# Joined state and V products in a chunked recurrence, a later rotation, three more held-back units and a norm's sum on TensorE

## The chip, the core and the metric

The kernel runs on one core of one Trainium2 chip, in one launch. The metric is the device time of that core in microseconds (us), as the median of several runs. Five engines work beside each other, each in its own order: TensorE (PE, its weight loads PEld), VectorE (DVE), ScalarE (ACT), GpSimd (POOL) and SyncE (SP), whose queue issues the DMAs.

## The reference

Two layers, each a feed-forward block, a mixer of three kinds of heads, and a second feed-forward block, each followed by a layer norm. 16 learned tokens lead 512 input tokens, so 528 positions are computed. Cut to what the change touches:

```python
for l in range(2):
    h = layer_norm(alpha * h + 0.5 * swiglu(h, w_ff1_in, w_ff1_out))
    h = layer_norm(alpha * h + mixer(h))      # gated DeltaNet | RWKV-7 | retention
    h = layer_norm(alpha * h + 0.5 * swiglu(h, w_ff2_in, w_ff2_out))

def rwkv7_step(S, r, w, k, v, a, b):          # one token, 4 heads of 64 x 64
    S = S * w + outer(S @ a, b) + outer(v, k)
    return S, S @ r
y = head_group_norm(y) + (sum(r * k * r_k) * v)   # the bonus, then times a gate

q, k = rotary(q), rotary(k)                   # retention: x1*cos - x2*sin, x1*sin + x2*cos
```

## The kernel before

The 528 positions are cut into half 0 (272) and half 1 (256). Activations stand as 8 blocks of 128 channels by positions. A dense product is a *unit*: one weight tile of 1024 x 128 is loaded (`load_w`, L150: a DMA into `raw`, then ScalarE copies the high part and VectorE subtracts it from the raw value, giving `whl`), and `mm3` (L160) runs 24 passes, high x high, high x low and low x high for each of 8 blocks. A unit of half 1 has 256 columns, of half 0 272. A float32 product that isn't split this way shows as two passes in the trace. Feed-forward units are `gate`, `up` and `ffo`; input units of the mixer `rt`, `ba`, `qkv`, `rw`, `z`; output units `out`.

The mixer works on "supers" of two chunks of 64 positions (the first of a layer is one chunk of 16). `rwkv_pre` prepares operands, `inverse_base` and `inverse_levels` invert a triangular matrix, `rwkv_chain` (L911) is the serial part, and `rwkv_post` normalises. In a step of the chain for a chunk, `pR` takes the product of the state with kappa (`kr[..., 0]`) and, accumulated, of V with the upper part of `Am` (`pR<-UV,Am`); `R` is its copy; `pu` multiplies by the inverse; `pSr` updates the state; `pyr` takes the state with r (`kr[..., 1]`) and then U and V together with the other half of `Am`. ScalarE copies `pyr` into `yv`. The layer's first chunk has no state yet.

`rt` units 0 and 1 are retention's q and k: the product goes into a bank of psA, ScalarE copies it to `rq`, a matmul with a fixed matrix makes the rotated copy `rot` in psA's other bank, and VectorE and GpSimd combine both with the two tables `tab`, which a DMA brings after the product.

`layer_norm` (L189): GpSimd sums the 8 blocks into `acc`; `pmean` is a matmul with ones; VectorE subtracts the mean from four pairs of blocks; ScalarE squares them; VectorE and GpSimd add the squares into one block; `pvar` sums over channels; a short chain of VectorE steps makes the inverse root, and `prs` spreads it.

What sets the order: the program is written down half by half, and a scheduler puts each engine's instructions into one fixed order from priorities and durations of its own model; tiles of a pool (psA, psB: 2 banks, psC: 3, and rings of named buffers in `RINGS`, L78) hold a new user back until the last one has ended. An engine then runs its list in order. In layer 0 the first feed-forward of half 1 is split: `u[:h]` (L1196, h = 13) runs before the mixer's input units of half 0, the rest beside the half-0 mixer, which fills TensorE while the chain waits.

Of the kernel before, what the change touches and what calls it, by code (L numbers as in the profile page):

```python
# [12 lines left out]
AF = mybir.ActivationFunctionType  # L13
# [22 lines left out]

_C = {}
_n = 0
for _name, _w in (("id", 128), ("u2", 128), ("mneg", 128), ("lvl", 2 * 64), ("rm", 128), ("rm0", 32),
                  ("u", 128), ("rot", 128), ("b2", 128), ("hm", 4), ("bm", 2), ("g128", 4), ("g16", 4)):  # L40
    _C[_name] = (_n, _n + _w)
    _n += _w
# [17 lines left out]
def body(ctx, tc, xT, w1i, w1o, w2i, w2o, win, wba, wout, par, wsm, wupx, cst, tab, out):  # L60
# [15 lines left out]


    RINGS = {  # L78
        "ws": (276, 5), "acc": (NMAX, 2), "dg": (NMAX, 2),
        "p2": (2 * NMAX, 15), "p1": (264, 8), "i2": (512, 5), "xr": (256, 2), "i1": (256, 2), "c2": (512, 2), "c1": (256, 2),  # L80
        "ti": (4, 16), "tp": (4, 18), "s6": (24, 2), "tf": (24, 10),
    }

# [15 lines left out]
    def bank(pool, name="ps"):  # L99
        return pool.tile([128, 512], F32, tag="bank", name=name)  # L100
# [13 lines left out]
    def tt(e, o, a, b, op):  # L114
        e.tensor_tensor(out=o, in0=a, in1=b, op=op)  # L115
# [13 lines left out]
    def mm(o, l, r, start=True, stop=True):  # L129
        PE.matmul(o, lhsT=l, rhs=r, start=start, stop=stop)  # L130
# [36 lines left out]

    S = {}

    nh, off = list(NH), [0, 0]  # L170

    def hv_(hf):
# [16 lines left out]
    def layer_norm(hf, l, j, last=False):  # L189
# [14 lines left out]
        for k in range(0, 8, 2):  # L204
            stt(hv[:, k: k + 2], bc(pm[:, :n], 1, (128, 2, n)), -1.0 / 1024, hv[:, k: k + 2], ALU.mult, ALU.add)
            sq = ring("p2", 2, n, name="sq")
            act(sq, hv[:, k: k + 2], AF.Square)
            sqs.append(sq)
            if k == 2:
                tt(V if end else G, sqs[0], sqs[0], sq, ALU.add)  # L210
# [4 lines left out]
        tt(V, sq[:, 0], sq[:, 0], sq[:, 1], ALU.add)  # L215
        for i in range(4):
# [153 lines left out]
    def in_units(l):  # L370
# [81 lines left out]
        def rt(i):  # L452
            def run(hf, w):
                n = nh[hf]
                ps = bank(psA, "rt")[:, :n]
                mm3(ps, w, S["hl", hf], 8)
                d = keep(hf, "rt")[:, i, :n]
                if i < 2:
                    q = ring("ws", n, name="rq")
                    act(q, ps, AF.Copy)  # L460
                    pr = bank(psA, "rot")[:, :n]
                    mm(pr, cs["rot"], q)
                    tb = [ring("ws", n, name="tab") for _ in range(2)]
                    for j in range(2):
                        nc.sync.dma_start(out=tb[j], in_=tab[hf, :, 2 * i + j, :n])
                    tt(V, d, pr, tb[1], ALU.mult)
                    tt(G, q, q, tb[0], ALU.mult)
                    tt(G, d, d, q, ALU.add)
                elif i < 4:
                    act(d, ps, AF.Copy)  # L470
                else:
                    silu2(d, ps, n)
            return (win[l, 19 + i], 8, run)

        def zz(i):
# [15 lines left out]
    def inverse_base(dg, dw, nch, Cn):  # L491
# [9 lines left out]

        def M(c, h):
            r = slice(64 * c, 64 * c + Cn)
            return Mg[r, h, 64 * c: 64 * c + Cn] if h < 4 else Am[h % 2][r, 2 * c + (h - 4) // 2, :Cn]

        def at(t, off, ap):
            return bass.AP(tensor=t.tensor, offset=t.offset + off, ap=ap)
# [5 lines left out]
        for c in range(nch):  # L513
            r = slice(64 * c, 64 * c + Cn)
            o = c * 8 * HS
            nc.sync.dma_start(out=at(md, o, [[Cn, Cn], [HS, 4], [1, Cn]]), in_=Mg[r, :, 64 * c: 64 * c + Cn])
            for e in range(2):
                nc.sync.dma_start(out=at(md, o + (4 + e) * HS, [[Cn, Cn], [2 * HS, 2], [1, Cn]]),
                                  in_=Am[e][r, 2 * c: 2 * c + 2, :Cn])
# [271 lines left out]
    def rwkv_pre(hf, si, d, pool):  # L791
# [7 lines left out]
        def pc(ap):  # L799
            return ap.rearrange("p j (c t) -> p j c t", c=nch)  # L800
# [42 lines left out]
        bb = ta  # L843
        stt(bb, ta, 1.0, kap, ALU.add, ALU.mult)
        tt(V, bb, bb, rec, ALU.mult)
        yield

        bk = ring("p2", 2, 2 * nch, w, name="bk")
# [14 lines left out]
        rkp = kap  # L863
        tt(G, rkp, r_, kp, ALU.mult)
        pb = bank(pool, "pb")[:, : 2 * n].rearrange("p (j t) -> p j t", j=2)
        for j in range(2):
            mm(pb[:, j], S["rk2"][:, j], rkp[:, j])
        bv = two("bv")
        for c in range(nch):
            cc, cv = slice(c * Cn, c * Cn + Cn), slice((nch - 1 - c) * Cn, (nch - c) * Cn)  # L870
            tt(V, bv[:, :, cc], pb[:, :, cc], v_[:, :, cv], ALU.mult)
        yield

        Am = []
        w2 = 2 * w
        rmask = cs["rm"] if nch == 2 else cs["rm0"]
        bkc = bk.rearrange("p j (c b) t -> p j c (b t)", c=nch)

        pA = [bank(pool, "pAr")[:w2, : nch * 4 * Cn].rearrange("p (q i) -> p q i", q=2 * nch) for _ in range(2)]
# [31 lines left out]
    def rwkv_chain(hf, si, d):  # L911
        s, n, nch, Cn, w = SUPERS[hf][si]
        w2 = 2 * w
        Am, UV, kr, bkt = d["Am"], d["UV"], d["kr"], d["bkt"]
        yv = ring("c1", 4, 64, name="yv")
        d["yv"] = yv
        for c in range(nch):
            r = slice(64 * c, 64 * c + Cn)
            vr = slice(w, w + Cn) if c == 0 else slice(0, Cn)
            Sb, first = S["Sr"], not (hf or si)  # L920
            pR = bank(psC, "pR")[:, :256]
# [8 lines left out]
            act(R[r], pR[r], AF.Copy)  # L930
            yield
# [3 lines left out]
            py = bank(psC, "pyr")[:, :256].rearrange("p (h d) -> p h d", h=4)  # L935
            if not first:
                for j in range(2):
                    mm(py[r, 2 * j: 2 * j + 2].rearrange("p h d -> p (h d)"), kr[:, j, c, 1], Sb[:, j], j == 0, False)
# [5 lines left out]
            for j in range(2):  # L944
                for e in range(2):
                    h = 2 * j + e
                    mm(py[r, h], Am[e][:w2, 2 * c + j, Cn: 2 * Cn], UV[:w2, c, 64 * h: 64 * h + 64],
                       first, first or h == 3)
            pc4 = bc(d["pcm"][:, c].rearrange("p j e -> p (j e)"), 2, (128, 4, 64))
            S24 = Sb.rearrange("p j (e d) -> p (j e) d", e=2)  # L950
            if not first:
                tt(V, Sb, Sb, pS, ALU.add)
                tt(V, S24, S24, pc4, ALU.mult)
            else:
                tt(V, S24, pS.rearrange("p j (e d) -> p (j e) d", e=2), pc4, ALU.mult)
            act(yv[r], py[r], AF.Copy)
            yield

    def rwkv_post(hf, si, d):
# [21 lines left out]
        tt(V, S["rt", hf][:, 4:6, sl], y, pg, ALU.mult)  # L981
        yield


# [191 lines left out]
    for l in range(L):  # L1176
# [67 lines left out]
def _consts():  # L1244
# [17 lines left out]
    put("rm", np.concatenate([j64[:, None] < k[None, :], j64[:, None] <= k[None, :]], 1))  # L1262
# [107 lines left out]
```

## Time and profile before

| | |
|---|---|
| median of 3 runs | 2441.68 us (2435.64 to 2444.03) |
| the profiled execution | 2435.65 us, span 2433.9 us |
| mean granted TensorE clock | 0.987 |
| busy: PE, DVE, ACT, POOL | 97%, 74%, 51%, 12% of the span |
| matmul passes in the trace | 19834 |

The profile is of one execution. Busy time of an engine is the time in which at least one of its instructions runs; matmuls are pipelined, so a pass shown as 0.28 us can follow the last one after 0.12 us, and the distance between two starts is what a pass costs. A row of a timeline merges equal instructions that follow each other. A number in square brackets at the end of a row is the engine's idle time ahead of it, with the instruction that ended the wait. Some per cent of matmul records can be missing. The granted clock of TensorE has two levels, 1.00 (2.4 GHz) and 0.50 (1.2 GHz).

### The profile page before, as it was taken

How to read it: one execution, taken by the hardware profiler on the slowest of the kernel's cores; microseconds unless marked ns; L12 is line 12 of the kernel's file. 1: busy time of each engine (PE TensorE's matmuls, PEld its weight loads, DVE VectorE, ACT ScalarE, POOL GpSimd, SP SyncE). 2: the span in 40 equal slices, each digit the busy share in tenths (PEclk: the TensorE clock that was granted, in tenths of full speed). 3: DMA queues.
4: the chain of work that ended last, by engine and by line, in shares of the span. 5: the costliest groups of instructions: out<-in, count | busy, mean ns of one | idle time of the engine just before them, and what ended most of it. 6: DMA issues, size and time to landing. Idle time of an engine off the chain costs nothing. (4 is left out here: it accounts for less than half of the span.)

```text
span 2433.9 us, 51363 instructions
## 1 busy us (share of the span) xinstructions
PE 2360.8 (97%) x19834; PEld 2270.8 (93%) x19834; DVE 1812.2 (74%) x4315; ACT 1229.7 (51%) x2821; POOL 297.0 (12%) x484
## 2 busy tenths in 40 slices
PE   9999999997999999999999999999998999999997
PEld 9999999996999999999999999899998999999997
DVE  6668687867788756976657779976688886677667
ACT  5445555534566335554444555544556653445444
POOL 1001112101223000300000003220022220010002
PEclk9999999998999999999999999999999999999998
DMA  6655544433454625555555554344455445355554
GB/s 233 209 171 166 187 163 135 147 113 110 147 171 150 174 88 168 166 173 182 180 177 181 193 163 142 119 138 124 153 170 191 157 148 155 122 164 174 191 169 134
DMA packets 169819, 389.24 MB, mean 160 GB/s; under 512 B 63750, under 2 KB 79720, under 8 KB 168936
## 3 DMA queue, kind: packets, MB, share of 16 engines
q1 hardware_dynamic: 169576, 385.97, 49.3%
q8 instruction: 156, 2.56, 0.4%
q14 instruction: 87, 0.71, 0.1%
HBM read 372.04 MB, written 13.88 MB: 159 GB/s over the span
## 5 line engine op out<-in xcount | busy, mean ns | idle before, releaser
L127 ACT ACTIVATE whl<-raw 128x512 fp32r<-128x512 f32 x1384 | 780.2, 614 | 627.5 <-PE ffo L165 198.3
L115 DVE TENSOR_TENSOR whl<-raw,whl 128x512 fp32r<-128x512 f32 x1384 | 949.4, 717 | 105.0 <-ACT whl L127 92.1
L165 PE MATMUL gate<-hi,whl 128*128 128x256 f32 (+1 forms) x2816 | 552.7, 287 | 6.3 <-DVE m L118 4.7
L165 PE MATMUL up<-hi,whl 128*128 128x256 f32 (+1 forms) x2816 | 552.6, 287 | 2.0 <-ACT whl L127 1.0
L165 PE MATMUL ffo<-ghi,whl 128*128 128x256 f32 (+1 forms) x2816 | 532.2, 286 | 3.4 <-DVE h L118 3.3
L165 PEld LDWEIGHTS gate<-hi,whl 128*128 128x128 f32 x2816 | 449.5, 189 | 12.1 <-DVE m L118 5.5
L165 PEld LDWEIGHTS up<-hi,whl 128*128 128x128 f32 x2816 | 450.2, 189 | 6.4 <-ACT whl L127 1.1
L165 PEld LDWEIGHTS ffo<-ghi,whl 128*128 128x128 f32 x2816 | 441.0, 188 | 9.8 <-DVE h L118 4.5
L165 PE MATMUL gate<-lo,whl 128*128 128x256 f32 (+1 forms) x1408 | 402.6, 286 | 0.6 <-DVE lo L115 0.6
L165 PE MATMUL up<-lo,whl 128*128 128x256 f32 (+1 forms) x1408 | 402.8, 286 | 0.0
L165 PE MATMUL ffo<-glo,whl 128*128 128x256 f32 (+1 forms) x1408 | 399.1, 284 | 0.0
L165 PEld LDWEIGHTS up<-lo,whl 128*128 128x128 f32 x1408 | 265.8, 189 | 2.2 <-issue 0.5
L165 PEld LDWEIGHTS gate<-lo,whl 128*128 128x128 f32 x1408 | 265.6, 189 | 2.2 <-DVE lo L115 1.1
L165 PEld LDWEIGHTS ffo<-glo,whl 128*128 128x128 f32 x1408 | 264.9, 188 | 1.0 <-issue 0.4
L127 ACT ACTIVATE tanh<-gate 128x256 f32<-128x256 f32 (+1 forms) x176 | 68.2, 388 | 219.3 <-PE gate L165 218.9
L118 DVE SCALAR_TENSOR_TENSOR h<-ffo,h 128x256 f32<-128x256 f32 (+1 forms) x192 | 81.2, 427 | 109.7 <-PE ffo L165 108.8
L118 DVE SCALAR_TENSOR_TENSOR m<-tanh,gate 128x256 f32<-128x256 f32 (+1 forms) x176 | 74.5, 423 | 116.0 <-ACT tanh L127 115.1
L165 PE MATMUL qkv<-hi,whl 128*128 128x272 f32 (+1 forms) x768 | 152.5, 290 | 1.9 <-ACT rk L127 1.9
L115 DVE TENSOR_TENSOR m<-m,up 128x256 f32<-128x256 f32 (+1 forms) x176 | 74.6, 424 | 96.9 <-PE up L165 96.4
L165 PEld LDWEIGHTS qkv<-hi,whl 128*128 128x128 f32 x768 | 122.5, 188 | 5.3 <-ACT rk L127 2.7
L165 PE MATMUL qkv<-lo,whl 128*128 128x272 f32 (+1 forms) x384 | 109.4, 285 | 0.0
L165 PE MATMUL out<-yhi,whl 128*128 128x256 f32 (+1 forms) x512 | 98.6, 291 | 7.4 <-DVE h L118 3.1
(326 smaller groups left out, 3221.4 us busy)
## 6 DMA issues: line engine op xcount, KB each, us to landing
raw<-w1i SPq DMA_DIRECT2D x176, 512.0 KB, 3.5
raw<-w2i SPq DMA_DIRECT2D x176, 512.0 KB, 3.4
raw<-win SPq DMA_DIRECT2D x116, 512.0 KB, 3.3
raw<-w1o SPq DMA_DIRECT2D x64, 512.0 KB, 3.3
raw<-w2o SPq DMA_DIRECT2D x64, 512.0 KB, 3.3
raw<-wout SPq DMA_DIRECT2D x32, 512.0 KB, 3.3
raw<-w1o SPq DMA_DIRECT2D x32, 384.0 KB, 3.1
raw<-w2o SPq DMA_DIRECT2D x32, 384.0 KB, 3.1
```

Of the source, the lines that this page charges most:

```text
L115: e.tensor_tensor(out=o, in0=a, in1=b, op=op)
L118: V.scalar_tensor_tensor(out=o, in0=a, scalar=s, in1=b, op0=op0, op1=op1)
L127: A.activation(out=o, in_=a, func=f, **kw)
L165: PE.matmul(ps, lhsT=w[:, a, k, :m], rhs=x[b][:, k, :n], start=(i == 0), stop=(i == 3 * nk - 1))
```

## The change

- **Recurrence.** `kr` holds kappa and r side by side, in the order (kappa, r) for chunk 0 and (r, kappa) for chunk 1, so that one product with the state gives 128 rows: 64 for `R` and 64 for y. The V product uses both halves of `Am` at once and accumulates into the same bank. ScalarE copies both parts out; `pyr` keeps only U's product, which VectorE adds to y. y and the bonus `bv` of the two chunks now stand in reversed order, which `rwkv_post` undoes in its last product. `Am` is masked chunk by chunk with shifted windows of a wider mask.
- **`rkp`**, the factor of the bonus, is made one step earlier.
- **Rotation.** The tables come in one DMA ahead of the unit's passes; the rotated product is written after the next unit's passes (`later`, `flush`) into a bank of psB.
- **Held-back units.** h = 10 for 13.
- **Last norm.** TensorE sums all eight blocks of squares for the last half of the last layer.
- **Rings.** `dg` one buffer for two, `c1` three for two, `rm` 64 columns wider.

```diff
-        "ws": (276, 5), "acc": (NMAX, 2), "dg": (NMAX, 2),
+        "ws": (276, 5), "acc": (NMAX, 2), "dg": (NMAX, 1),
...
+    def later(fn):
+        S.setdefault("later", []).append(fn)
+    def flush():
+        for fn in S.pop("later", ()):
+            fn()
...
+            if end:
+                for kk in range(2):
+                    for i in range(4):
+                        mm(pv[:w, i: i + 1], sq[:, kk, i * w: i * w + w], ones[:, 0:1], k + kk + i == 0, k + kk == 7 and i == 3)
+                continue
...
                 if i < 2:
                     q = ring("ws", n, name="rq")
                     act(q, ps, AF.Copy)
-                    pr = bank(psA, "rot")[:, :n]
-                    mm(pr, cs["rot"], q)
-                    tb = [ring("ws", n, name="tab") for _ in range(2)]
-                    for j in range(2):
-                        nc.sync.dma_start(out=tb[j], in_=tab[hf, :, 2 * i + j, :n])
-                    tt(V, d, pr, tb[1], ALU.mult)
-                    tt(G, q, q, tb[0], ALU.mult)
-                    tt(G, d, d, q, ALU.add)
+                    flush()
+                    def rotate():
+                        pr = bank(psB, "rot")[:, :n]
+                        mm(pr, cs["rot"], q)
+                        tt(V, d, pr, tb[:, 1], ALU.mult)
+                        tt(G, q, q, tb[:, 0], ALU.mult)
+                        tt(G, d, d, q, ALU.add)
+                    later(rotate)
...
-        tt(G, kr[:, :, :, 0], pc(kap), Pt[:, :, :, 0:Cn], ALU.mult)
-        tt(G, kr[:, :, :, 1], pc(r_), Pt[:, :, :, 1:], ALU.mult)
+        for c in range(nch):
+            tt(G, kr[:, :, c, c], pc(kap)[:, :, c], Pt[:, :, c, 0:Cn], ALU.mult)
+            tt(G, kr[:, :, c, 1 - c], pc(r_)[:, :, c], Pt[:, :, c, 1:], ALU.mult)
...
-            tt(V, a[:w2], pA[e], bc(rmask[:w2, : 2 * Cn], 1, (w2, 2 * nch, 2 * Cn)), ALU.mult)
+            for c in range(nch):
+                q2 = slice(2 * c, 2 * c + 2)
+                tt(V, a[:w2, q2], pA[e][:, q2], bc(rm[c][:w2, : 2 * Cn], 1, (w2, 2, 2 * Cn)), ALU.mult)
...
-            for j in range(2):
-                if not first:
-                    mm(pR[r, 128 * j: 128 * j + 128], kr[:, j, c, 0], Sb[:, j], True, False)
-                for e in range(2):
-                    h = 2 * j + e
-                    mm(pR[r, 64 * h: 64 * h + 64], Am[e][vr, 2 * c + j, :Cn], UV[vr, c, 64 * h: 64 * h + 64],
-                       first, first or e == 1)
+            if not first:
+                for j in range(2):
+                    mm(pR[:, 128 * j: 128 * j + 128], kr[:, j, c].rearrange("p a t -> p (a t)"), Sb[:, j], j == 0, False)
+            o, ka = (r, slice(0, Cn)) if first else (slice(0, 128), slice(0, 2 * Cn))
+            for h in range(4):
+                mm(pR[o, 64 * h: 64 * h + 64], Am[h % 2][vr, 2 * c + h // 2, ka], UV[vr, c, 64 * h: 64 * h + 64], first, first or h == 3)
             act(R[r], pR[r], AF.Copy)
+            if not first:
+                act(y, pR[ry], AF.Copy)
...
+            py = bank(psC, "pyr")[:, :256]
+            for h in range(4):
+                mm(py[ry, 64 * h: 64 * h + 64], Am[h % 2][ur, 2 * c + h // 2, ra], UV[ur, c, 64 * h: 64 * h + 64])
...
-            act(yv[r], py[r], AF.Copy)
+            if first:
+                act(y, py[ry], AF.Copy)
+            else:
+                tt(V, y, y, py[ry], ALU.add)
...
-            h = 13
+            h = 10
```

The order on TensorE at the end of the first feed-forward of half 1 in layer 0, before (`pot`, `pyt` and `pgate` are the mixer's tail, `pmean`, `pvar` and `prs` the norm of half 1, `out` the output units of half 0):

```order
L130 MATMUL pSr<-UV,rk 128x128 x2
L130 MATMUL pyr<-UV,Am 64x64 x4
L765 MATMUL pot<-cst,on 128x128 x4
L130 MATMUL pmean<-acc,ones 128x256
L130 MATMUL pvar<-ones,sq 64x1 x4
L973 MATMUL pyt<-cst,yn 128x128 x2
L130 MATMUL pgate<-sg,wsm 128x128 x2
L130 MATMUL prs<-diag,ones 128x256
L165 MATMUL out<-yhi,whl 128x272 x2
```

And now, from the last `ffo` pass on (between `pot` and this row stand 108 `ffo` passes):

```order
L165 MATMUL ffo<-ghi,whl 128x256
L130 MATMUL pmean<-acc,ones 128x256
L1003 MATMUL pyt<-cst,yn 128x128 x2
L130 MATMUL pgate<-sg,wsm 128x128 x2
L130 MATMUL pvar<-ones,sq 64x1 x4
L165 MATMUL out<-yhi,whl 128x272 x2
L165 MATMUL out<-ylo,whl 128x272
```

The mixer's tail now comes before `pvar`, and `prs` follows 27 `out` passes later. The same tail in layer 1 had 111 `ffo` passes between `pot` and `pyt` and none between `pgate` and `out`; now 7 `up` and 117 `ffo` passes stand there, and 27 `ffo` passes behind `pgate`.

A step of the recurrence on TensorE, in the half-0 mixer of layer 0, before (`pR` holds what the products leave, `Sr` the state, `UV` the u and v rows; `up` is the feed-forward of the other half):

```order
L130 MATMUL pR<-Sr,kr 64x128
L130 MATMUL pR<-UV,Am 64x64 x2
L130 MATMUL pR<-Sr,kr 64x128
L130 MATMUL pR<-UV,Am 64x64 x2
L165 MATMUL up<-hi,whl 128x256
```

And now, with the same neighbours on either side:

```order
L165 MATMUL up<-hi,whl 128x256 x2
L130 MATMUL pR<-Sr,kr 128x128 x2
L130 MATMUL pR<-UV,Am 128x64 x4
L165 MATMUL up<-lo,whl 128x256
L165 MATMUL up<-hi,whl 128x256 x2
```

The two blocks' state passes now stand together and ahead of all four UV passes, each twice as wide in its output. The row `pyr<-Sr,kr 64x128 x2`, which followed each later `pu` before, is gone. At the last norm the row `pvar<-ones,sq 64x1 x4` became `pvar<-ones,sq 64x1 x32`.

## Rows read from the trace of the kernel before

**Rows 1.** The page, busy time of each engine, share of the span, instructions

```profile
PE 2360.8 (97%) x19834; PEld 2270.8 (93%) x19834; DVE 1812.2 (74%) x4315; ACT 1229.7 (51%) x2821; POOL 297.0 (12%) x484
```

**Rows 2.** Windows: length, busy us (count) by engine, granted clock, DMA share, GB/s

```profile
550.00:600.00 50.00, 39.42 (x359) 36.21 (x358) 38.48 (x103) 21.75 (x53) 8.75 (x13) 0.93 0.38 126
...
1100.00:1150.00 50.00, 50.00 (x411) 50.00 (x410) 31.36 (x58) 22.86 (x45) 0.00 (x0) 1.00 0.55 179
```

**Rows 3.** Timeline of TensorE: start, length, line, out<-in, count, [idle before]

```profile
584.79 0.65 PE L130 MATMUL pyr<-Sr,kr 128*64 128x128 f32 x4
...
586.18 0.60 PE L130 MATMUL pSr<-UV,rk 128*128 128x128 f32 x4
586.72 0.68 PE L130 MATMUL pyr<-UV,Am 128*64 128x64 f32 x8
587.33 0.66 PE L765 MATMUL pot<-cst,on 128*128 128x128 f32 x4
587.82 0.62 PE L130 MATMUL pmean<-acc,ones 128*128 128x256 f32 x2
...
607.14 0.59 PE L165 MATMUL out<-ylo,whl 128*128 128x272 f32 x1 [2.35 <-DVE ylo L115]
```

**Rows 4.** The same for VectorE, same stretch

```profile
590.87 2.47 DVE L118 SCALAR_TENSOR_TENSOR h<-pmean,h 128x512 f32<-128x512 f32 x4
```

**Rows 5.** Timeline of TensorE in the rotation units of half 1, both layers

```profile
639.98 0.70 PE L130 MATMUL rot<-rq,cst 128*128 128x256 f32 x2 [0.47 <-ACT rq L127]
...
646.30 0.38 PE L165 MATMUL rt<-hi,whl 128*128 128x256 f32 x1 [2.46 <-DVE rt L115]
...
1844.33 0.58 PE L165 MATMUL rt<-hi,whl 128*128 128x256 f32 x1 [3.39 <-DVE rt L115]
```

**Rows 6.** Timeline of TensorE at the mixer's tail in layer 1

```profile
2119.14 0.66 PE L765 MATMUL pot<-cst,on 128*128 128x128 f32 x4
...
2135.21 0.41 PE L973 MATMUL pyt<-cst,yn 128*128 128x128 f32 x2 [2.29 <-DVE yn L115]
...
2138.49 0.80 PE L165 MATMUL out<-yhi,whl 128*128 128x256 f32 x2 [1.99 <-ACT yhi L127]
```

**Rows 7.** Timeline: a norm at full clock, and the last one

```profile
226.15 0.60 PE L130 MATMUL pvar<-ones,sq 128*68 128x1 f32 x8
...
2417.39 2.42 ACT L127 ACTIVATE sq<-h 128x512 f32<-128x512 f32 x4 [4.87 <-DVE h L118]
...
2421.87 0.98 PE L130 MATMUL pvar<-ones,sq 128*64 128x1 f32 x8 [5.31 <-DVE sq L115]
```

**Rows 8.** Windows behind three waits of TensorE

```profile
648.00:654.00 6.00, 6.00 (x33) 6.00 (x33) 2.64 (x11) 1.42 (x3) 0.00 (x0) 0.50 0.28 90
1843.00:1848.50 5.50, 4.17 (x19) 4.13 (x19) 2.23 (x4) 0.00 (x0) 4.31 (x7) 0.50 0.53 176
2136.00:2142.00 6.00, 4.01 (x18) 3.49 (x17) 1.11 (x2) 1.10 (x3) 0.83 (x2) 0.50 0.32 99
```

**Rows 9.** Timeline of TensorE in one recurrence step

```profile
546.25 0.43 PE L130 MATMUL pR<-Sr,kr 128*64 128x128 f32 x2
546.61 0.44 PE L130 MATMUL pR<-UV,Am 64*64 64x64 f32 x4
546.98 0.43 PE L130 MATMUL pR<-Sr,kr 128*64 128x128 f32 x2
```

**Rows 10.** Timeline of TensorE: bonus factor and a product with the wide load

```profile
1617.21 0.71 PE L130 MATMUL pb<-kap,rk 128*128 128x128 f32 x4 [1.39 <-POOL kap L115]
1617.85 1.16 PE L130 MATMUL pAr<-kr,bk 64*128 64x128 f32 x8
```

**Rows 11.** The page, groups: busy us, mean ns, idle before

```profile
L115 DVE TENSOR_TENSOR whl<-raw,whl 128x512 fp32r<-128x512 f32 x1384 | 949.4, 717 | 105.0 <-ACT whl L127 92.1
```

**Rows 12.** Timeline of GpSimd and VectorE in the rotation units, layer 0

```profile
641.51 1.23 POOL L115 TENSOR_TENSOR rt<-rt,rq 128x256 f32<-128x256 f32 x1
...
642.06 2.37 DVE L115 TENSOR_TENSOR whl<-raw,whl 128x512 fp32r<-128x512 f32 x2
```

More of the change, by code (lines that the diff above doesn't have):

```diff
@@ L38 @@
 _n = 0
-for _name, _w in (("id", 128), ("u2", 128), ("mneg", 128), ("lvl", 2 * 64), ("rm", 128), ("rm0", 32),
+for _name, _w in (("id", 128), ("u2", 128), ("mneg", 128), ("lvl", 2 * 64), ("rm", 192), ("rm0", 32),
                   ("u", 128), ("rot", 128), ("b2", 128), ("hm", 4), ("bm", 2), ("g128", 4), ("g16", 4)):
@@ L78, in body @@
     RINGS = {
-        "ws": (276, 5), "acc": (NMAX, 2), "dg": (NMAX, 2),
-        "p2": (2 * NMAX, 15), "p1": (264, 8), "i2": (512, 5), "xr": (256, 2), "i1": (256, 2), "c2": (512, 2), "c1": (256, 2),
+        "ws": (276, 5), "acc": (NMAX, 2), "dg": (NMAX, 1),
+        "p2": (2 * NMAX, 15), "p1": (264, 8), "i2": (512, 5), "xr": (256, 2), "i1": (256, 2), "c2": (512, 2), "c1": (256, 3),
         "ti": (4, 16), "tp": (4, 18), "s6": (24, 2), "tf": (24, 10),
@@ L208, in layer_norm @@
             sqs.append(sq)
+            if end:
[3 more added lines that the diff above has]
+                continue
             if k == 2:
-                tt(V if end else G, sqs[0], sqs[0], sq, ALU.add)
+                tt(G, sqs[0], sqs[0], sq, ALU.add)
             if k == 6:
@@ L214, in layer_norm @@
         sq = sqs[0]
-        tt(V, sq[:, 0], sq[:, 0], sq[:, 1], ALU.add)
-        for i in range(4):
+        if not end:
+            tt(V, sq[:, 0], sq[:, 0], sq[:, 1], ALU.add)
+        for i in range(0 if end else 4):
             mm(pv[:w, i: i + 1], sq[:, 0, i * w: i * w + w], ones[:, 0:1])
@@ L454, in run @@
                 n = nh[hf]
+                d = keep(hf, "rt")[:, i, :n]
+                if i < 2:
+                    tb = ring("p2", 2, n, name="tab")
+                    nc.sync.dma_start(out=tb, in_=tab[hf, :, 2 * i: 2 * i + 2, :n])
                 ps = bank(psA, "rt")[:, :n]
                 mm3(ps, w, S["hl", hf], 8)
-                d = keep(hf, "rt")[:, i, :n]
                 if i < 2:
@@ L472, in run @@
                     silu2(d, ps, n)
+                if i >= 2:
+                    flush()
             return (win[l, 19 + i], 8, run)
@@ L503, in M @@
             r = slice(64 * c, 64 * c + Cn)
-            return Mg[r, h, 64 * c: 64 * c + Cn] if h < 4 else Am[h % 2][r, 2 * c + (h - 4) // 2, :Cn]
+            return Mg[r, h, 64 * c: 64 * c + Cn] if h < 4 else Am[h % 2][r, 2 * c + (h - 4) // 2, c * Cn: c * Cn + Cn]
         def at(t, off, ap):
@@ L518, in inverse_base @@
                 nc.sync.dma_start(out=at(md, o + (4 + e) * HS, [[Cn, Cn], [2 * HS, 2], [1, Cn]]),
-                                  in_=Am[e][r, 2 * c: 2 * c + 2, :Cn])
+                                  in_=Am[e][r, 2 * c: 2 * c + 2, c * Cn: c * Cn + Cn])
         B = ring("i1", BS, BS, name="B")[:parts]
@@ L845, in rwkv_pre @@
         tt(V, bb, bb, rec, ALU.mult)
+        rkp = rec
+        tt(G, rkp, r_, kp, ALU.mult)
         yield
@@ L861, in rwkv_pre @@
         yield
-        rkp = kap
-        tt(G, rkp, r_, kp, ALU.mult)
         pb = bank(pool, "pb")[:, : 2 * n].rearrange("p (j t) -> p j t", j=2)
@@ L870, in rwkv_pre @@
             cc, cv = slice(c * Cn, c * Cn + Cn), slice((nch - 1 - c) * Cn, (nch - c) * Cn)
-            tt(V, bv[:, :, cc], pb[:, :, cc], v_[:, :, cv], ALU.mult)
+            tt(V, bv[:, :, cv], pb[:, :, cc], v_[:, :, cv], ALU.mult)
         yield
@@ L875, in rwkv_pre @@
         w2 = 2 * w
-        rmask = cs["rm"] if nch == 2 else cs["rm0"]
+        rm = [cs["rm"][:, 64 - 64 * c: 192 - 64 * c] if nch == 2 else cs["rm0"] for c in range(nch)]
         bkc = bk.rearrange("p j (c b) t -> p j c (b t)", c=nch)
@@ L920, in rwkv_chain @@
             Sb, first = S["Sr"], not (hf or si)
+            ry = slice(64 - 64 * c, 128 - 64 * c) if nch == 2 else r
+            ra = slice((1 - c) * Cn, (2 - c) * Cn)
+            ur = slice(0, w2) if first else r
             pR = bank(psC, "pR")[:, :256]
-            for j in range(2):
-                if not first:
-                    mm(pR[r, 128 * j: 128 * j + 128], kr[:, j, c, 0], Sb[:, j], True, False)
-                for e in range(2):
-                    h = 2 * j + e
-                    mm(pR[r, 64 * h: 64 * h + 64], Am[e][vr, 2 * c + j, :Cn], UV[vr, c, 64 * h: 64 * h + 64],
-                       first, first or e == 1)
+            if not first:
[4 more added lines that the diff above has]
+                mm(pR[o, 64 * h: 64 * h + 64], Am[h % 2][vr, 2 * c + h // 2, ka], UV[vr, c, 64 * h: 64 * h + 64], first, first or h == 3)
             R = ring("c1", 256, name="R")
             act(R[r], pR[r], AF.Copy)
+            y = yv[ry].rearrange("p h d -> p (h d)")
+            if not first:
+                act(y, pR[ry], AF.Copy)
             yield
@@ L934, in rwkv_chain @@
                 mm(pu[r, 64 * h: 64 * h + 64], d["X"][r, h], R[r, 64 * h: 64 * h + 64])
[L935 to L938, printed above, removed]
             act(UV[r, c], pu[r], AF.Copy, scale=-1.0)
@@ L943, in rwkv_chain @@
                 mm(pS[:, j], bkt[:w2, 2 * c + j], UV[:w2, c, 128 * j: 128 * j + 128])
[L944 to L948, printed above, removed]
+            py = bank(psC, "pyr")[:, :256]
+            for h in range(4):
+                mm(py[ry, 64 * h: 64 * h + 64], Am[h % 2][ur, 2 * c + h // 2, ra], UV[ur, c, 64 * h: 64 * h + 64])
             pc4 = bc(d["pcm"][:, c].rearrange("p j e -> p (j e)"), 2, (128, 4, 64))
@@ L980, in rwkv_post @@
             mm(pg[:, j], S["wsm"][64:128, 128 * j: 128 * j + 128], sg[64:128])
-        tt(V, S["rt", hf][:, 4:6, sl], y, pg, ALU.mult)
+        nch, Cn = SUPERS[hf][si][2:4]
+        for c in range(nch):
+            cc, cv = slice(c * Cn, c * Cn + Cn), slice((nch - 1 - c) * Cn, (nch - c) * Cn)
+            tt(V, S["rt", hf][:, 4:6, s + c * Cn: s + c * Cn + Cn], y[:, :, cv], pg[:, :, cc], ALU.mult)
         yield
@@ L1261, in _consts @@
     put("lvl", lv.reshape(128, -1))
-    put("rm", np.concatenate([j64[:, None] < k[None, :], j64[:, None] <= k[None, :]], 1))
+    le = j64[:, None] <= k[None, :]
+    put("rm", np.concatenate([le, j64[:, None] < k[None, :], le], 1))
     r0, k16 = np.arange(64) % 32, np.arange(16)
```

## The prediction

> **What bounds the kernel now.** I read the busy times first. TensorE is busy 97% of the 2433.9 us span [rows 1], so a pass taken off its stream counts in full, and work on another engine counts only where TensorE waits for it. Second came the windows of 50 us: an undisturbed one holds 411 passes, 0.122 us each, while 550 to 600 holds 359 and only 39.4 us of busy TensorE [rows 2]. Third, the timelines of the thin windows, where the idle time before a row names who was waited for. Four places stand out.
>
> At the end of the first feed-forward of half 1 in layer 0, TensorE finishes `pmean` at 588 and runs its next dense row at 607.14 [rows 3]. In between VectorE does two things at once: the norm of half 1, whose four subtractions start only at 590.87 [rows 4], and the tail of the half-0 mixer, on which `pyt`, `pgate` and then `out` depend. In the rotation units of half 1 the third `rt` unit waits 2.46 us in layer 0 and 3.39 us in layer 1, both times for VectorE's `rt<-rot,tab` [rows 5]: the bank of the rotated product is one of psA's two. In layer 1 the same mixer tail makes `pyt` wait 2.29 us and `out` 1.99 us [rows 6]. Last, the closing norm [rows 7].
> Behind three of these waits (both rotations and the tail in layer 1) the granted clock stands at 0.50 (1.2 GHz): all through 648 to 654, 1843 to 1848.5 and 2136 to 2142 [rows 8]. In the last of these 18 passes take 4.01 us, 0.22 each, so a microsecond at that clock does the work of about 0.55, and a stretch of six loses some 2.5 us.
>
> **Part 1, the joined products.** A recurrence step of a later chunk (16 of them: two layers, four pairs of chunks each) had, in passes of TensorE, twice (state 2, V 4) at 546.98 - 546.25 = 0.73 us, together 1.47 [rows 9]; the state product of the output, 0.6 (0.65 with the tail); and the output's own eight, 587.33 - 586.72 = 0.61 [rows 3]. That is 2.68. Now one state product of 128 columns does both: four passes 128*128, like `pSr`, 586.72 - 586.18 = 0.54 [rows 3]. The V product becomes eight passes that load 128 columns from 64 rows. The trace has such a load in `pAr`: eight in 1.16 us to the end of the last, 1.1 without its tail [rows 10], though with 128 moving columns where these have 64; the old narrow ones cost 2 x (546.98 - 546.61) = 0.74 for eight [rows 9]. I take 1.0, near `pAr`, whose load has the same shape. The output keeps eight passes, 0.61. Sum 2.15, a gain of 0.53 x 16 = 8.5 us; by the bounds (1.16 and 0.74 for the wide product) 6 to 13.
>
> Beside it VectorE takes over the sum into y (ScalarE's copy of y merely moves forward), the mask of `Am` and the product with the gate come in two pieces, and GpSimd makes `kr` in four pieces for two. A sum of 256 columns I put at 0.4 us, an estimate from the mean of 0.717 us for a split of 512 [rows 11]; 16 of them are 6.7 us, all pieces together some 12 us, on engines that are busy 74% and 12% [rows 1]. The feed-forward passes between the steps hide them; without that cover they would cost those 12. I put 2 us on the path.
>
> **Part 2, three more held-back units.** 72 passes, 72 x 0.122 = 8.8 us, leave the front of layer 0 and run beside the half-0 mixer. At the front two units instead of five now cover the first norm; the two waits there stay about as they were, since the first `rt` unit needs the bank that the second gate needed. At the other end, by the order, 108 `ffo` passes (13.2 us) stand between `pot` and `pmean`, where there were none, so the tail's own norm runs beside them. From `pmean` on I count: 0.6 for it, 2.5 for the four subtractions [rows 4], 1.0 for the end of the head norm, then `pyt`, `pgate` 1.2, sums of squares and `pvar` 2, split of the gated output before `out` 1.5: about 9 instead of 607.14 - 587.82 = 19.3 [rows 3]. Gain 10. Bounds: 0, if VectorE's queue is the whole of the 19.3, and 15, if only TensorE's own 4 us stay.
>
> **Part 3, the later rotation.** Its bank now comes from psB, its matmul stands a unit later and the tables are asked for before the unit's passes. That takes away the two waits, 5.9 us, the wait for the copy `rq` (0.47 before the second `rot` [rows 5], eight rotations, some 3 us), and, where the clock row follows the idling, twice 2.5. Together 14. What is late next is the weights: VectorE still makes four subtractions, the sums of squares and one split pair per unit there. I leave 3 us of waiting and take 11; bounds 0 and 14, no loss, because the order asks for the tables no later than before.
> The trace shows what may keep it: two splits take 2.37 us from 642.06 on, where GpSimd works on its rotation products, against a mean of 2 x 0.717 [rows 11, 12]. The Trainium skill (SBUF — State Buffer, "SBUF: two separate sides") calls the port pair of VectorE and GpSimd an exclusive lock, on which a VectorE operation with two SBUF inputs waits for a GpSimd one; that agrees with these rows and speaks against this part, because GpSimd's products stay beside the splits. By that rule alone the units would wait for weights as long as they did for the bank.
>
> **Part 4, the tail in layer 1.** The order puts 124 passes (15.1 us) between `pot` and `pyt`, which were 16.07 us apart [rows 6], and 27 `ffo` passes (3.3 us) before `out`, over the 1.99. One microsecond of wait stays; with half a clock stretch back I take 5, bounds 0 and 7.
>
> **Part 5, the last norm.** VectorE's four sums go, and 64 one-column passes come for eight. The first squares are there at 2418.0, the last at 2419.8 [rows 7]. At 226.15, at full clock, eight such passes take 0.60 with the tail of the last, 0.06 a step; at 2421.87, at half clock, 0.98, 0.11 a step. So 64 end at 2422.1 or at 2425.1, against 2422.85 now: -0.7 to +2.3. TensorE idles before them as it did, so I take +1.
> The Trainium skill (TensorE: Matmul & The Clock Gate, "What's actually happening") has the low clock as the default that activity lifts; the rows on either side of 654 agree, but whether one-column passes are enough activity no row shows. By it the loss is 2.3.
>
> **Part 6, the early `rkp`.** `pb` waited 1.39 us for it [rows 10], and once more alike. `kr` is now last on GpSimd and `pAr` takes over most of the wait: 1 us, bounds 0 and 3.
>
> **The sum.** -8.5 - 10 - 11 - 5 + 1 - 1 + 2 = -32.5 us, against the profiled execution's 2435.65 (span 2433.9 and 1.75 around it): 2403. The median of the runs shown, 2441.68, lies 6.0 higher, so it becomes **2409**.
>
> **Rivals.**
> *The rotation wait turns into a wait for weights.* Part 3's gain falls to nothing: 2420. For it: the stretched splits [rows 12]. Against: psA's bank was named as the releaser both times [rows 5].
> *The end of the mixer stays bound by VectorE.* The norm, the head norm and the splits still meet in one queue, and TensorE only waits elsewhere: parts 2 and 4 fall from 15 to 4, 2420. For it: the four subtractions alone start 3 us behind `pmean` [rows 3, 4]. Against: 108 passes now lie ahead of it, beside the head norm.
> *The change does nothing that counts.* The passes saved were hidden behind waits and the waits move along: 2438, no difference.
> *Slower: a bank held by VectorE.* The output's bank `pyr` was emptied by ScalarE, and now by a VectorE sum that stands in order behind weight splits; psC has three banks, and the next user on TensorE waits. Two stretched splits are 2.4 us [rows 12]; 16 steps of it are 38 us, and the change loses from 2.1 us a step on: 2447. Against it: feed-forward passes stand between the steps, and the order puts the sum right behind its product.
>
> **How the numbers follow.** Forecast 0.50, first rival 0.20, second 0.15, no effect 0.08, slower 0.07. What this measurement can tell from no change is 0.3%, 7 us, that is below 2434 and above 2449. All but the last two cases are faster; some of both of these spill over: faster 0.86, same 0.09, slower 0.05. The range runs from 2393, where most upper bounds hold (about 49 us), to 2432, where two rivals hold together.
>
> **What would show it.** Right: `pR` as four passes of 128*128 and eight of 64*128 in about 1.5 us and no state product of `pyr`; less than 10 us from `pmean` to the stream of `out` in layer 0; no wait before the third `rt` unit above 1 us and no stretch of 0.50 in the rotation units; no 1.99 before `out` in layer 1. Wrong: `rt` or `up` waiting for VectorE's `whl` in those units, `pu` or `pot` waiting for VectorE's y, or the gap behind `pmean` still near 19. Most of all it would be wrong if the saved passes left TensorE's span where it is.

## The result

| | us | ratio to before |
|---|---|---|
| before, 4 runs beside the changed kernel | 2438.79 | |
| changed, 4 runs | 2408.34 (2406.62 to 2411.15) | 0.9877, 95% interval 0.9859 to 0.9896 |
| changed, 4 runs more, another session | 2413.03 (2409.08 to 2414.04) | 0.9891, 0.9871 to 0.9910 |
| forecast | 2409 (2393 to 2432) | |

The change takes 1.1 to 1.2% off. The time came out where it was forecast, but several terms of the sum did not: their errors cancelled.

**The profile after.** Columns as in the groups of before. The page, busy times and share of the span:

```profile
PE 2347.6 (98%) x19826; PEld 2270.2 (94%) x19826; DVE 1823.5 (76%) x4351; ACT 1231.0 (51%) x2821; POOL 305.0 (13%) x500
```

VectorE and GpSimd have 11 and 8 us more work, TensorE 13 us less; the span fell from 2433.9 to 2404.5 us.

TensorE in one recurrence step, against [rows 9]:

```profile
556.97 0.28 PE L165 MATMUL up<-lo,whl 128*128 128x256 f32 x1
557.09 0.60 PE L130 MATMUL pR<-Sr,kr 128*128 128x128 f32 x4
557.62 1.10 PE L130 MATMUL pR<-UV,Am 64*128 64x64 f32 x8
558.66 0.50 PE L165 MATMUL up<-hi,whl 128*128 128x256 f32 x2
```

The four state passes take 557.62 - 557.09 = 0.53 us and the eight wide ones 1.04. The first state pass starts 0.12 us behind a dense pass, as a dense pass would.

TensorE at the end of layer 0's first feed-forward, against [rows 3]:

```profile
580.54 0.28 PE L165 MATMUL ffo<-ghi,whl 128*128 128x256 f32 x1
583.98 0.70 PE L130 MATMUL pmean<-acc,ones 128*128 128x256 f32 x2 [3.17 <-POOL acc L115]
588.86 0.66 PE L1003 MATMUL pyt<-cst,yn 128*128 128x128 f32 x2 [4.18 <-DVE yn L115]
589.45 1.22 PE L130 MATMUL pgate<-sg,wsm 64*128 64x128 f32 x4
590.71 0.98 PE L130 MATMUL pvar<-ones,sq 128*64 128x1 f32 x8
592.42 0.82 PE L165 MATMUL out<-yhi,whl 128*128 128x272 f32 x2 [0.73 <-ACT yhi L127]
```

From `pmean` to the unbroken stream of `out` 8.4 us pass instead of 19.3, but `pmean` itself now waits 3.17 us for GpSimd's last addition into `acc`. Before, two passes of `out` had already run ahead of the wait that [rows 3] shows at 607.14, which the prediction left out; to these it was 16.2 us:

```profile
603.98 0.82 PE L165 MATMUL out<-yhi,whl 128*128 128x272 f32 x2 [0.78 <-ACT yhi L127]
```

The rotation in half 1 of both layers, and what comes behind it, against [rows 5]:

```profile
626.86 0.59 PE L130 MATMUL rot<-rq,cst 128*128 128x256 f32 x2
630.13 0.59 PE L130 MATMUL rot<-rq,cst 128*128 128x256 f32 x2
...
656.77 0.39 PE L165 MATMUL rw<-hi,whl 128*128 128x256 f32 x1 [4.61 <-ACT conv L127]
...
1818.79 0.59 PE L130 MATMUL rot<-rq,cst 128*128 128x256 f32 x2
1822.06 0.59 PE L130 MATMUL rot<-rq,cst 128*128 128x256 f32 x2
...
1848.91 0.58 PE L165 MATMUL rw<-hi,whl 128*128 128x256 f32 x1 [4.09 <-ACT conv L127]
```

No wait is left before `rot` or the third `rt` unit. The wait for ScalarE's `conv`, which empties the bank of a `qkv` unit, has grown. Before it was 2.58 us in layer 0, and in layer 1 there was none, only 1.09 us for ScalarE's `baT` and 0.41 for its `rk`:

```profile
672.62 0.39 PE L165 MATMUL rw<-hi,whl 128*128 128x256 f32 x1 [2.58 <-ACT conv L127]
```

The last norm, against [rows 7]:

```profile
2382.92 0.59 PE L130 MATMUL pmean<-acc,ones 128*128 128x256 f32 x2
2383.60 0.70 PE L130 MATMUL pmean<-h,ones 128*128 128x256 f32 x2
2387.03 6.34 PE L130 MATMUL pvar<-ones,sq 128*64 128x1 f32 x64 [2.74 <-ACT sq L127]
2395.89 1.19 PE L130 MATMUL prs<-diag,ones 64*128 64x256 f32 x2 [2.51 <-DVE diag L115]
```

**A ledger by stage.** I cut both traces at the same program points (starts of `pmean`, `pyt`, `pot`), took the difference in time, and where dense passes had moved from one stage to another took them out at 0.118 or 0.127 us each, the usual distances of passes of 256 and 272 columns. "Net" also leaves out what the half clock cost: for each pass in a stretch at 0.50, the time to its successor beyond the median of its form at full clock, at most one such median and 0.03 us. Where exactly a stage is cut moves a row by up to 0.4 us here, and by up to 0.9 in the experiments.

| stage, us | before to changed | net of the half clock | forecast |
|---|---|---|---|
| front and first norm | -0.4 | -0.4 | 0 |
| rotation and input units, four times | -9.2 | -6.9 | -11 |
| half mixers up to `pot`, four times | -14.0 | -14.2 | -6.5 and -1 |
| tail and `out`, layer 0 | -3.0 | -2.5 | -10 |
| tail and `out`, layer 1 | -5.7 | -3.7 | -5 |
| last norm | +2.8 | +0.7 | +1 |
| sum, with 0.1 elsewhere | -29.5 | -26.8 | -32.5 |

### The profile page after: what moved, and what is told of

Its sections match the earlier page's. It is cut to its first block, busy times and chain, and to the rows that moved or that the text cites. A ratio compares the mean times of both kernels' runs of the same rounds, so it can differ in the third digit from the quotient of the medians.

```text
span 2404.5 us, 51375 instructions
## 1 busy us (share of the span) xinstructions
PE 2347.6 (98%) x19826; PEld 2270.2 (94%) x19826; DVE 1823.5 (76%) x4351; ACT 1231.0 (51%) x2821; POOL 305.0 (13%) x500
## 4 chain that ended last, share of the span: by engine, by line
PE 86%; DVE 8%; ACT 2%; DMA 1%; issue 1%; POOL 1%; SPq 0%; POOLq 0%; DVEq 0%; ACTq 0%
PE ffo L165 20%; PE gate L165 20%; PE up L165 20%; PE qkv L165 6%; PE rw L165 3%; PE out L165 3%; DVE whl L115 3%; PE rt L165 2%; DVE h L118 1%; PE pR L130 1%; PE pz L130 1%; PE px L130 1%; DVE lo L118 1%; PE z L165 1%; PE po L130 1%
## 5 line engine op out<-in xcount | busy, mean ns | idle before, releaser
L165 PEld LDWEIGHTS ffo<-ghi,whl 128*128 128x128 f32 x2816 | 440.7, 188 | 10.1 <-DVE h L118 3.7
```

Source lines behind the costliest of these rows:

```text
L165: PE.matmul(ps, lhsT=w[:, a, k, :m], rhs=x[b][:, k, :n], start=(i == 0), stop=(i == 3 * nk - 1))
```

## The experiments

Ratios are to the kernel before, from the runs beside it. "Net" time is the end of TensorE's work less the loss at half clock, as above: 2411.5 before, 2384.6 changed. The time of one kernel can't be told from that of the changed one where their intervals overlap: that holds for h = 13, 9 and 8, the old closing norm, the bank alone and the late `rkp`. What is said of these rests on one profile each, and two profiles of the changed kernel itself (last experiment) differ by 0.9 us net in all and by up to 1 us in a stage.

**The closing norm alone undone**

```diff
-            if end:
-                for kk in range(2):
...
+                tt(V if end else G, sqs[0], sqs[0], sq, ALU.add)
...
+        for i in range(4):
```

> The changed kernel with the closing norm's sums back on VectorE, all else as changed. Theory of the stage ledger: the 64 one-column passes at half clock cost 2.8 us from the end of pmean to prs, so this kernel takes 2405.5 us, ratio to before 0.9864, and prs follows pmean by 10.2 us instead of 13.0. Rival (the forecast's term): they cost 1 us, 2407.3 us, 0.9871, prs 12 us behind pmean.

Measured 2409.67, 0.9886 (0.9872 to 0.9901): no difference that the times can tell. The trace can: `prs` follows the first `pmean` by 10.2 us instead of 13.0 (TensorE's timeline):

```profile
2389.31 0.59 PE L130 MATMUL pmean<-acc,ones 128*128 128x256 f32 x2
...
2396.00 0.98 PE L130 MATMUL pvar<-ones,sq 128*64 128x1 f32 x8 [5.32 <-DVE sq L115]
2399.49 1.19 PE L130 MATMUL prs<-diag,ones 64*128 64x256 f32 x2 [2.51 <-DVE diag L115]
```

So this part costs 2.8 us in the changed kernel's first profile. The ledger's theory, that the passes ran at half clock, holds only for 51 of the 64: the granted clock fell while they ran (Part 5 below). Where it falls differs. In the eight profiles with this norm `prs` follows `pmean` by 11.8 to 13.9 us, in the six with the old one by 10.2 in all, so the price is 1.7 to 3.8 us, and 1.8 in the changed kernel's second profile. The rest of this kernel is ordered as in the changed one, and yet its last `pmean` comes 6.4 us later: up to there the half clock cost 15.7 us and not 9.7 (last experiment).

**h = 13**

```diff
-            h = 10
+            h = 13
```

> The changed kernel with h = 13, so that 72 passes go back to the front of layer 0. Forecast's term: 10 us slower than the changed kernel, 2418 us, ratio to before 0.9916. Theory of the ledger: only 3 us lie in the tail of layer 0's half-0 mixer and some 2 in the mixer itself, 2413.5 us, 0.9897. A third view, by which fewer front units gained nothing and the wait only stands elsewhere: 2408, 0.9877.

Measured 2412.13, 0.9897 (0.9882 to 0.9912); net 2389.7, 5.1 above the changed kernel. The three stages of layer 0 that the units touch are 4.7 us longer (2.1 net). So the three units are worth 5 us at most, half of the forecast.

**Everything but the joined products**

The edit takes the recurrence's part out of the changed kernel, `rkp` excepted:

```diff
-                    mm(pR[:, 128 * j: 128 * j + 128], kr[:, j, c].rearrange("p a t -> p (a t)"), Sb[:, j], j == 0, False)
+                    mm(pR[r, 128 * j: 128 * j + 128], kr[:, j, c, 0], Sb[:, j], True, False)
...
+                    mm(py[r, 2 * j: 2 * j + 2].rearrange("p h d -> p (h d)"), kr[:, j, c, 1], Sb[:, j], j == 0, False)
```

> The kernel before with every other part of the change but without the joined products: rotation, h = 10, rkp and the closing norm as changed. Forecast's term: the joined products are worth 6.5 us with their pieces on VectorE and GpSimd, so 2415 us, ratio to before 0.9902. Theory A: their passes alone, 8.5 us with no cost beside them, 2417 us, 0.9911. Theory B: all of the 14 us that the four mixers lost up to pot is theirs, as shorter steps let the dense passes in sooner: 2422 us, 0.9931.

Measured 2419.83, 0.9938 (0.9917 to 0.9960); net 2396.8, 12.2 above the changed kernel. By stages the four mixers are some 14 to 15 longer (12.5 to 13.4 net) and nothing else differs by more than 1.6: theory B.

**The old rotation in the changed kernel**

```diff
-                    def rotate():
-                        pr = bank(psB, "rot")[:, :n]
...
+                    pr = bank(psA, "rot")[:, :n]
+                    mm(pr, cs["rot"], q)
+                    tb = [ring("ws", n, name="tab") for _ in range(2)]
```

> The changed kernel with the rotation of before. Forecast's term: 11 us, so 2419 us, ratio to before 0.9919, with the waits of 2.5 and 3.4 us before the third rt unit of half 1 back. Theory of the ledger: 9.2 us, 2417.5 us, 0.9913, and the waits of 4.8 and 4.3 us for the conv on ScalarE before the first rw unit fall back to some 2 us. Rival: the later rotation only moves the wait, within 4 us of the changed kernel, below 2412 us.

Measured 2423.8, 0.9950 (0.9933 to 0.9968), more than anyone said. The four rotation stages are some 7 us longer, somewhat under the ledger's 9.2, and the wait for `conv` falls back to 2.57 us in layer 0. The other 10 lie elsewhere, 7.3 of them in layer 1's half-1 mixer and its tail, which the scheduler ordered differently: 128 `ffo` passes stand between `pot` and `pyt`, none behind `pgate`, and two waits stand in TensorE's timeline that the changed kernel hasn't:

```profile
1975.45 0.70 PE L924 MATMUL pbk<-cst,bk 128*128 128x128 f32 x4 [2.64 <-DVE Am L115]
...
2122.90 0.80 PE L165 MATMUL out<-yhi,whl 128*128 128x256 f32 x2 [3.06 <-ACT yhi L127]
```

**h = 8**

```diff
-            h = 10
+            h = 8
```

> The changed kernel with h = 8. In its order the tail of layer 0's half-0 mixer has 7 up and 100 ffo passes between pot and pyt, and 44 ffo and 33 out passes between pgate and pmean, as layer 1 has. Theory: the three waits there (3.3, 4.3 and 0.9 us) and the half clock behind them go, some 10 us; at the front 48 passes fewer cover the first norm, so the wait before the first rt unit grows from 1.9 us by up to 5.6. Net 4 us faster than the changed kernel: 2404 us, ratio to before 0.986. Rival: VectorE's queue only moves the waits to out, and the front costs 5.6: 2414 us, 0.990.

Measured 2413.66, 0.9890 (0.9867 to 0.9914). Both halves of the theory came true, and a third thing ate the gain. In the tail of layer 0 `pyt` and `pmean` wait no more, and it ends 10.0 us shorter; the front is 5.2 longer, where `rt` waits for the normalised half 0. But the norm of half 1 now reaches into the `rt` units of half 1, and these lose 5.8 us (2.2 net); the half-0 mixer and layer 0's second tail lose 2.7 and 3.3 (1.2 and 1.9 net), which no experiment explains. Net the whole is 1.6 above the changed kernel. TensorE's timeline:

```profile
593.78 0.59 PE L130 MATMUL pmean<-acc,ones 128*128 128x256 f32 x2
...
618.25 0.39 PE L165 MATMUL rt<-lo,whl 128*128 128x256 f32 x1 [2.16 <-DVE lo L118]
```

**The joined products alone**, in the kernel before

```diff
+                    mm(pR[:, 128 * j: 128 * j + 128], kr[:, j, c].rearrange("p a t -> p (a t)"), Sb[:, j], j == 0, False)
...
+                tt(V, y, y, py[ry], ALU.add)
```

> The kernel before with the joined products alone (and the ring sizes that go with them). Forecast's term: 6.5 us, 2431 us against 2437, ratio 0.9973. Theory A: passes (8.5 us) and switches between dense passes and passes of a smaller tile, 0.09 us each, some 2 us: 10.4 us, 0.9957. Theory B: all of the 12.6 us that taking it out of the changed kernel cost, 0.9948, if the parts add up.

Measured 2422.53, 0.9937 (0.9915 to 0.9959); net -11.8, near theory B; the times alone fit A as well. So the term doesn't hang on the other parts. It is made up of 11.9 in the mixers (net; 10.1 with the clock) and 3.6 in the tail of layer 1, whose new order (117 `ffo` passes before `pyt`, 27 behind `pgate`) comes with this part, less 3.6 that two feed-forwards lost. Two waits for GpSimd's bonus factor are in it, 2.17 and 1.87 us, as TensorE's timeline has them:

```profile
471.42 0.71 PE L130 MATMUL pb<-kap,rk 128*128 128x128 f32 x4 [2.17 <-POOL kap L115]
...
1971.29 0.71 PE L130 MATMUL pb<-kap,rk 128*128 128x128 f32 x4 [1.87 <-POOL kap L115]
```

**The later rotation alone**, in the kernel before

```diff
-                    pr = bank(psA, "rot")[:, :n]
...
+                        pr = bank(psB, "rot")[:, :n]
...
+                    later(rotate)
```

> The kernel before with the later rotation alone. Forecast's term: 11 us, ratio to before 0.9955. Taking it out of the changed kernel cost 16.6 us: if the parts add up, 0.9932. Theory C: some 6 of these came from the order that the old rotation met in the changed kernel (the waits for Am and for out in layer 1), and alone it gives what the stages show, 9.2 us, 0.9962.

Measured 2434.81, 0.9986 (0.9974 to 0.9997), below every theory. Its four stages gain 7.4 us (5.8 net), somewhat under theory C; 6.3 of it (3.5 net) is lost again at places that the change doesn't touch, by small new waits and the half clock. And the wait for `conv` is there in full in TensorE's timeline:

```profile
668.80 0.58 PE L165 MATMUL rw<-hi,whl 128*128 128x256 f32 x1 [4.62 <-ACT conv L127]
```

**The bank of psB without the postponement**

```diff
-                    later(rotate)
+                    rotate()
```

> The changed kernel with the rotation's matmul right behind its copy in the program, in the bank of psB, with the tables early: only the postponement is gone. In the order the matmul now follows 20 to 26 passes behind its copy in half 1 and 24 in half 0 of layer 0's front none. Theory bank: the wait was for psA's bank, and the time stays within 3 us of the changed kernel, 2407 to 2411, ratio 0.987 to 0.989. Theory postponement: the waits for the copy, 0.6 us each, and the third unit's wait come back, 2416 us or more, 0.991.

Measured 2411.82, 0.9889 (0.9869 to 0.9909), 0.8 us over the range of theory bank; the rotation stages are as in the changed kernel within 0.7 us (net), and no wait of half 1's is back. So the written postponement isn't needed. What freed them is the bank, with the early tables (no run takes the two apart): in half 1 the scheduler itself puts the matmul 20 to 26 passes later once the bank doesn't hold it back. Net the whole kernel is 4.4 us above the changed one, 3.0 of it in layer 1's half-0 mixer and 1.4 in layer 0's second tail; why is open.

**`rkp` at its old place**

```diff
-        rkp = rec
-        tt(G, rkp, r_, kp, ALU.mult)
...
+        rkp = kap
+        tt(G, rkp, r_, kp, ALU.mult)
```

> The changed kernel with rkp made where it was, behind kr. Forecast's term: 1 us, ratio to before 0.988. Theory from the run of the joined products alone, in which pb waited 2.3 us in layer 0 and 2.0 us in layer 1 for GpSimd (none of it in the changed kernel): with kr in four pieces the old place costs 4 us and, where the clock halves behind the waits, up to 3 more: 2412 us, 0.990.

Measured 2415.66, 0.9907 (0.9886 to 0.9927); net +4.0. `pb` waits 1.57 us (1607.5) and 0.51 us (1545.5); more comes from an order that has 61 `ffo` passes before `pmean` in layer 0's tail, where the waits sum to 12.2 us (4.27, 5.97 and 1.93) instead of 8.1 (3.17, 4.18 and 0.73). The price is as in the theory, its place only in part.

**Joined products and rotation, nothing else**

```diff
-            h = 10
+            h = 13
```

and `rkp` and the closing norm as before.

> The kernel before with the joined products and the later rotation, and nothing else of the change. Theory 1, the parts add up as measured alone (15 and 3 us): 2418 us, ratio to before 0.992. Theory 2, the rotation is worth what its own stages show in every pair of traces, 7.4 to 9.2 us, and the rest of the 16 us that its removal cost was the order in layer 1: 2413 us, 0.990. Theory 3, beside the joined products it is worth all 16: 2406 us, 0.987.

Measured 2423.95, 0.9933 (0.9912 to 0.9954), none of the three: by the time the rotation adds nothing to the joined products. Net it adds 5.8, in its four stages 8.0. Its profile has twelve stretches at half clock, where that of the joined products alone has eight, and loses 6.7 us more in them.

**h = 9 and the old closing norm**

```diff
-            h = 10
+            h = 9
```

with the first experiment's edit.

> The changed kernel with h = 9 and the closing norm's sums back on VectorE, as the candidate for the best. The norm gives back 2.8 us; at the front 24 passes fewer cover the first norm, so the wait before the first rt unit grows by up to 2.9 us or, if it was for psA, by nothing; in the tail of layer 0 136 ffo passes stand between pot and pyt: the wait for pmean's sum goes, 3 us. Together 2404 us, ratio to before 0.986; rival: as fast as the changed kernel, 0.9877.

Measured 2408.82, 0.9880 (0.9858 to 0.9903); net 2383.1, 1.5 below the changed kernel. The norm gives back 2.8 us, the tail of layer 0 3.3; the front takes 1.5 and the half-0 mixer 2.6. As fast as the changed kernel, no better that the times can show.

**The changed kernel again**, with no edit

> The changed kernel itself once more, in company with the three others: ratio to before 0.9877 within 0.002. Its waits should be the same to 0.1 us, while the stretches at half clock may stand elsewhere: the time net of them within 1 us of the first profile, the stretches' own loss anywhere from 12 to 17 us.

Measured 2413.03, 0.9891 (0.9871 to 0.9910). The waits are the same (3.17, 4.18, 4.61 and 4.09 us in the first profile, 3.16, 4.17, 4.61 and 4.08 in this one), and from 8 to 584 us the two traces agree within 0.05. The last passes end 7.0 us apart; net 0.9. The difference is the clock, with 6.2 us of it. One stretch of 6.7 us in the first profile of the changed kernel, as the windows have it (the last columns are granted clock, DMA share, GB/s):

```profile
1574.50:1581.20 6.70, 6.70 (x58) 6.16 (x57) 5.95 (x34) 5.75 (x23) 0.00 (x0) 1.00 0.07 10
```

The same window in this one:

```profile
1574.50:1581.20 6.70, 6.70 (x33) 6.16 (x32) 3.12 (x19) 3.06 (x17) 0.35 (x2) 0.50 0.23 78
```

33 passes instead of 58, with TensorE busy throughout in both. All in all the half clock cost 12.4 us in the first profile and 18.6 in this one, over the 17 expected, against 15.1 in that of before: of the 29.5 us between the first two profiles 2.6 are the clock's.

## Why the prediction was right, and where it was not

**The sum.** -32.5 was forecast; the medians lie 30.4 us apart (2438.79 - 2408.34), in the second session 23.4 (2436.41 - 2413.03). The nested kernels split the change without remainder, net of the clock: joined products -11.8, rotation on top -5.8, all the rest on top -9.3, together -26.9. That 2409 was met so closely is luck twice over: terms off in both directions cancelled, and it also owes to the median of before, which was 2441.68 in three runs and 2436 to 2439 in all later ones.

**Part 1, the joined products: passes right, total too small.** `pR` and `pyr` together fell from 43.0 to 34.5 us (without the layers' first chunks), the 8.5 of the forecast; a wide product takes 1.04 where 1.0 was taken. The 2 us for the pieces on VectorE and GpSimd didn't show: the dense passes hide them. What the sum missed is the switch: a pass that doesn't fill the 128 x 128 array starts 0.09 us late behind a dense one. Behind a dense pass the distance is 92 ns over the usual in the median of 9 groups of `pR<-Sr,kr` before, and 1 ns in 13 after, since the joined product fills the array. The same step in the kernel without the joined products:

```profile
558.37 0.28 PE L165 MATMUL gate<-hi,whl 128*128 128x256 f32 x1
558.59 0.43 PE L130 MATMUL pR<-Sr,kr 128*64 128x128 f32 x2
```

0.22 us to the successor there, 0.12 above. With the six `pyr` groups that stood alone it makes some 1.6 us. The Trainium skill (TensorEngine Tiling (Array Packing), "Key Properties") says that changing the tiling mode drains TensorE; these rows agree, with 0.09 us. Another 0.6 us lie behind those six groups: the first pass of `po`, a full one, takes 0.21 us to its successor behind `pyr` and 0.11 behind `pot`, as it stands now. About 1.5 of the 12.2 us stay without a place.

**Part 2, the held-back units: the step that failed.** "Gain 10" rests on 108 `ffo` passes taking 13.2 us before `pmean`, and 9 us behind it. The 9 were 8.4. But from `pot` to `pmean` 18.2 us passed (565.76 to 583.98): 1.5 more for the passes, and 3.17 for `acc`, whose last addition on GpSimd (1.1 us) stands behind VectorE's last `h`, itself queued behind splits. Behind `pmean`, the `out` stream took 3 us longer than before, with `prs` and two small waits in it. The stage gave 3.0, and putting the units back cost 4.7 in the stages that they touch. So what failed is the overlap: the 108 passes ended before the sum into `acc` was there, and `pyt` then waited 4.18 us for VectorE, which had the norm and the head norm in one queue. The second rival, VectorE's queue at the mixer's end, was closer to layer 0 than the forecast; in layer 1 it was wrong.

**Part 3, the rotation: waits right, the clock's share too large.** The 11 were some 6 us of waits (5.9 and 3, less 3) and 5 of half clock. The named waits went, and net of the clock the four stages gained 5.4 to 8 us in each of four comparisons, as the 6 say. Of the clock's 5 some 2 came in the first profile of the changed kernel and none in the second. The clock no longer stands at 0.50 at 648 and 1843 [rows 8], but it does behind the new waits, for 3.4 us each in the first profile and for 6.8 each in the second. With the clock the stages gained some 9 us in the first and 5 in the second, and 4.3 to 7.4 in the three other comparisons. The 3 us left "for weights" were really 4.61 and 4.09 for `conv`: by the rows of VectorE and ScalarE the earlier passes run into the norm of half 0, whose products and `lo` and `hi` steps lie ahead of `conv` in both queues:

```profile
646.66 3.35 DVE L118 SCALAR_TENSOR_TENSOR h<-h,par,prs 128x272 f32<-128x272 f32 x8
...
653.30 2.21 ACT L127 ACTIVATE h<-h,par 128x272 f32<-128x272 f32 x5
...
656.25 0.47 ACT L127 ACTIVATE conv<-qkv,par 128x256 f32<-128x256 f32 x1
```

The wait stands at 4.6 us in each of the profiles with the later rotation, and at 2.6 or less in those without. That is the first rival's form with another wait; that the norm is the cause was read, not tried. VectorE's splits beside GpSimd's products are still stretched (its timeline, two splits against 2 x 0.716):

```profile
634.00 2.67 DVE L115 TENSOR_TENSOR whl<-raw,whl 128x512 fp32r<-128x512 f32 x2
```

The Trainium skill (SBUF — State Buffer, "SBUF: two separate sides") has the two engines block each other at a shared port pair; the row agrees. But no pass waited for these weights.

**Part 4** was 5 and is 3.7 net, 5.7 with the clock. All of it came with the joined products alone.

**Part 5** was +1 and is +2.8, 0.5 over its bound, in one profile and +1.8 in the other. The passes were forecast from the first squares on, 2.8 us behind `pmean`. They started 4.1 us behind it (2387.03), when by ScalarE's row three of the four squares were there (2385.13 + 3/4 of 2.42). The first 13 took 0.06 us each; then the granted clock fell while they ran back to back, and the rest took 0.11 us each, to the end at 2393.37. TensorE in windows (the last columns are granted clock, DMA share, GB/s):

```profile
2387.00:2387.80 0.80, 0.77 (x14) 0.80 (x14) 0.00 (x0) 0.55 (x1) 0.00 (x0) 0.98 0.00 0
2387.80:2393.40 5.60, 5.57 (x54) 5.49 (x52) 0.00 (x0) 0.00 (x0) 0.00 (x0) 0.50 0.00 0
```

In the second profile 34 passes came before the fall. The forecast took one level for all 64 and had no case for a fall on the way. The Trainium skill (TensorE: Matmul & The Clock Gate, "What's actually happening") names activity as what lifts the clock; these passes, back to back, did not keep it up.

**Part 6**, the early `rkp`, was 1 and is some 4 net by one profile, 2.1 of it in waits of `pb`: with `kr` in four pieces the old place costs more than it did before, which the joined products alone show (2.17 and 1.87 us, against 1.39 and 1.11 before).

**The slower rival** did not come: in no trace does `pu`, `pot` or `pSr` wait long for y.

## What to carry to other kernels

Count array switches, not only passes: in these traces a product that fills the 128 x 128 array slips between dense passes for nothing, and a narrower one costs 0.09 us more. Where a scheduler makes the order, taking a part out and adding it alone can differ by 10 us (rotation: 2.3 and 13.4 net), so price parts by the stages that they touch and by nested kernels. Moving work to cover one wait brings the next queue's wait forward; read who is second in that queue before booking the gain.

## What was not expected of the hardware

The same program, with the same waits to 0.1 us, ran 7.0 us longer in one profile than in another, because the clock halved at other places or for longer, once while TensorE was busy throughout. That is as much as single parts of this change are worth, so two profiles can't be compared by their spans alone.
